# Attention of a decoder trunk on one Trainium2 core: score and value products of 256 columns as three passes over high and low parts, instead of plain fp32

## The chip, the core and the metric

The kernel runs on one core of a Trainium2 chip, as one launch. The metric is the device time of the whole launch in microseconds (us). Before the change it is 2285.92 us, the median of 3 runs from 2285.37 to 2287.04. A view of the profile names the engines so: PE is TensorE's matmuls and PEld its weight loads, DVE is VectorE, ACT is ScalarE, POOL is GpSimd, SP the queue that issues most DMAs.

## What is computed

256 tokens of width 2048 go through an attention mixer, an MLP, a state-space mixer and a second MLP, each with an RMS norm before it and a residual sum behind it. The change is in the attention mixer alone. What matters of its reference:

```python
q = (rms_norm(c_q, q_norm_g) @ w_uq).reshape(B, S, MLA_HEADS, QK_HEAD_DIM)      # 16 heads of 192
kv = (rms_norm(c_kv, kv_norm_g) @ w_ukv).reshape(B, S, MLA_HEADS, QK_NOPE_DIM + V_HEAD_DIM)
...
q = rms_norm(q, qn_g); k = rms_norm(k, kn_g)      # then rope on 64 of the 192 columns
s = jnp.einsum('bqhd,bkhd->bhqk', q_blk, k) * scale
mask = k_pos[None, :] <= q_pos[:, None]
p = jax.nn.softmax(jnp.where(mask, s, -jnp.inf), axis=-1)
return jnp.einsum('bhqk,bkhd->bqhd', p, v)
```

There are two blocks of 128 queries. The first sees 128 keys, the second 256, so that a head has score products of 128 and of 256 columns.

## The kernel before, in words

**Weights in two parts.** Nearly all matmul work of the kernel multiplies activations with weights, and both are held as two fp32r numbers, a high part (the value cut to fp32r) and a low part (the rest). A product is three passes: high by high, low by high, high by low (L339, L340, L343 in `block`; L616 to L618 in the MLPs). The parts of every weight chunk are made on the chip while the kernel runs: `halves` has ACT copy the chunk to fp32r (L102, tile `wh`) and DVE subtract that copy from the chunk (L103, `wl`). `Flow.convert` keeps this three chunks ahead of PE. So ACT and DVE have a steady load from the weights, beside what a mixer asks of them.

**The attention stage.** The 16 heads go in 8 units of two heads. The loop over the units in `mla_body` (L1018 and on) writes the work of several units into one another. Round u issues, in this order on PE: the query projection of unit u+1 (`s0q`, a block of 384 columns), the transposes of unit u-1's keys (`s1(u-1, "k")`), the key/value projection of unit u (`s0kv`, 512 columns) with the transposes of unit u-2's softmax in its middle (`s3`), the scores of unit u-1 (`s2`), the value products of unit u-2 (`s4`) and the transposes of unit u's queries (`s1(u, "q")`). Round 7 has a block of the output projection in place of `s0q`. PE keeps exactly the written order. A scheduler sets the order on ACT, DVE and POOL.

Between the stages a unit's data walks through the other engines:

- `q_stats`, `q_norm`: ACT squares and sums the projection (L296), POOL adds and takes the power -1/2 (L289, L290; called the root below), DVE scales it to `qn` (L887). `q_rope` on POOL turns 64 columns (L798 to L801) and copies `qn` by a DMA to fp32r words `qw`.
- `s0kv`, `k_norm`: the same for the keys: L296, the root on POOL, then DVE scales to `kn` (L916) and ACT adds the scaled rope part (L918). The values `v` are copied by ACT (L907).
- `s1`: PE transposes into PSUM banks, and DVE or ACT copies them out (L944, L946, L948) to plain fp32 tiles `qT` and `kT`. POOL clears the unused halves of the query tile (L927, L928).
- `s2`: per head, two products of 128 columns and two of 256 (L961, L962), plain fp32. DVE adds the mask and takes the maximum (L965), scales it (L967), ACT takes the exponential (L971), DVE the reciprocal (L972) and the product with it (L975).
- `s3`: three transposes per head, copied out by DVE (L987) for one head and ACT (L989) for the other.
- `s4`: per head one product of 256 columns (L997) and one of 128 (L998), plain fp32. `split_out` then makes the high part (ACT, L299) and the low part (DVE, L300) of the result for the output projection.

**Banks.** Transposes, scores and value products take their PSUM banks by turns from two pools, `yp` and `sm`, of two banks each, so that every fourth request gets the same bank again. The second bank of the key transposes is the one that `s4` of the round before wrote, and it is free once L300 has read it. Tiles of `xtp` (8) are shared by queries, keys, softmax and its transpose, four per unit.

Of the kernel before, what the change touches and what calls it, by code (L numbers as in the profile page):

```python
# [28 lines left out]
P = 128  # L29
# [185 lines left out]
class Trunk:  # L215
# [610 lines left out]
    def mla_body(self, mp, gain):  # L826
        nc, d = self.nc, self.d
        cq = [mp.tile([P, 4, 256], F32R, name=f"cq{i}") for i in range(2)]
        ckv = [mp.tile([P, 4, 256], F32R, name=f"ckv{i}") for i in range(2)]
        mk = mp.tile([P, 256], F32, name="mk")  # L830

        def setup():
            nc.gpsimd.memset(mk[:, 0:P], 0.0)
            nc.gpsimd.tensor_copy(mk[:, P:256], self.cst[:, C_MQ:C_MQ + P])
            self.rope_tables(mp)

# [2 lines left out]
        accs = self.block([("ain", "q", q) for q in range(4)], xT)  # L839
# [58 lines left out]

        def s0kv(u, mid=None):
            accs = self.block([("ukv", u)], ckvT, mid=mid)  # L900
            v = mp.tile([P, 2, 2, P], F32, tag="v", name=f"v{u}", bufs=3)
            ssq = self.stat(4)
            for t in range(2):
                for h in range(2):
                    self.square_sum(accs[t][:, h * P:(h + 1) * P], ssq[:, 2 * t + h:2 * t + h + 1], HD ** -0.5)
            for t in range(2):
                nc.scalar.activation(v[:, t].rearrange("p h f -> p (h f)"), accs[t][:, 256:512], AF.Copy)  # L907
            U[u]["kv"], U[u]["kr"], U[u]["v"] = accs, self.root(ssq, krss, 4), v

        def k_norm(u):  # L910
            accs, r = U[u]["kv"], U[u]["kr"]
# [9 lines left out]
        def s1(u, name):  # L921


            src, words = U[u][name + "n"], U[u].get(name + "w")
            dst = self.ktile(self.xtp, F32)
            if name == "q":
                nc.gpsimd.memset(dst[64:128, 2], 0.0)  # L927
                nc.gpsimd.memset(dst[0:64, 3], 0.0)  # L928
            for i in range(2):
                b = self.bank()  # L930
                parts = 2 - i
                for j in range(parts):
                    for t in range(2):
                        o = j * 256 + t * P
                        k = (2 * i + j) * P
                        if words is not None and (i, t) != (1, 1):
                            nc.tensor.transpose(b.bitcast(F32R)[:, o:o + P], words[:, t, k:k + P], self.ident_r)
                        else:
                            nc.tensor.transpose(b[:, o:o + P], src[:, t, k:k + P], self.ident)
                v = b[:, :parts * 256].rearrange("p (k n) -> p k n", k=parts)  # L940
                if i and name == "q":
                    for h in range(2):
                        r = slice(64 * h, 64 * h + 64)
                        nc.scalar.activation(dst[r, 2 + h], b[r, 0:256], AF.Copy)  # L944
                elif (i == 0) == (name == "q"):
                    nc.vector.tensor_copy(dst[:, 2 * i:2 * i + parts], v)  # L946
                else:
                    nc.scalar.activation(dst[:, 2 * i:2 * i + parts], v, AF.Copy)  # L948
            U[u][name + "T"] = dst

        def s2(u):
            qT, kT = U[u]["qT"], U[u]["kT"]
            p = self.ktile(self.xtp, F32).rearrange("p a b -> p (a b)")
            mx, nm, sm, rc = self.stat(4), self.stat(4), self.stat(4), self.stat(4)
            spans = ((0, P), (P, 384))
            for h in range(2):
                b = self.bank()
                q0, q1 = qT[:, h], qT[:, 2 + h]
                k0, k1 = kT[:, h], kT[:, 2]
                for o, n in ((0, P), (P, 256)):  # L960
                    nc.tensor.matmul(b[:, o:o + n], q0[:, o:o + P], k0[:, :n], start=True, stop=False)  # L961
                    nc.tensor.matmul(b[:, o:o + n], q1[:, o:o + P], k1[:, :n], start=False, stop=True)  # L962
                for i, (a, z) in enumerate(spans):
                    j = 2 * h + i
                    nc.vector.tensor_tensor_reduce(p[:, h * 384 + a:h * 384 + z], b[:, a:z], mk[:, 256 - (z - a):], 1.0, -3.0e38,  # L965
                                                   ALU.add, ALU.max, mx[:, j:j + 1])
                nc.vector.tensor_scalar(nm[:, 2 * h:2 * h + 2], mx[:, 2 * h:2 * h + 2], -SCALE, None, ALU.mult)  # L967
                for i, (a, z) in enumerate(spans):
                    j = 2 * h + i
                    v = p[:, h * 384 + a:h * 384 + z]  # L970
                    nc.scalar.activation(v, v, AF.Exp, bias=nm[:, j:j + 1], scale=SCALE, accum_out=sm[:, j:j + 1])  # L971
                nc.vector.reciprocal(rc[:, 2 * h:2 * h + 2], sm[:, 2 * h:2 * h + 2])  # L972
                for i, (a, z) in enumerate(spans):
                    j = 2 * h + i
                    nc.vector.tensor_scalar(p[:, h * 384 + a:h * 384 + z], p[:, h * 384 + a:h * 384 + z], rc[:, j:j + 1],  # L975
                                            None, ALU.mult)
            U[u]["p"] = p

        def s3(u):
            p = U[u]["p"]  # L980
            pT = self.ktile(self.xtp, F32).rearrange("p a b -> p (a b)")
            for h in range(2):
                b = self.bank()
                for i in range(3):
                    nc.tensor.transpose(b[:, i * P:(i + 1) * P], p[:, h * 384 + i * P:h * 384 + (i + 1) * P], self.ident)
                if h == 0:
                    nc.vector.tensor_copy(pT[:, 0:384], b[:, 0:384])  # L987
                else:
                    nc.scalar.activation(pT[:, 384:768], b[:, 0:384], AF.Copy)  # L989
            U[u]["pT"] = pT  # L990

        def s4(u):
            pT, v = U[u]["pT"], U[u]["v"]
            b = self.bank()
            for h in range(2):
                o = h * 256
                nc.tensor.matmul(b[:, o:o + 256], v[:, 0, h], pT[:, h * 384:h * 384 + 256], start=True, stop=False)  # L997
                nc.tensor.matmul(b[:, o + P:o + 256], v[:, 1, h], pT[:, h * 384 + 256:h * 384 + 384], start=False, stop=True)  # L998
# [609 lines left out]
```

## Time and profile before

| | |
|---|---|
| time of the runs | 2285.92 us median, 2285.37 to 2287.04 |
| the profiled execution, its own time | 2286.35 us |
| its span in the profile | 2284.5 us |
| granted TensorE clock | 1.0 of full speed |
| busy share of the span | PE 100%, PEld 83%, DVE 84%, ACT 61%, POOL 12% |
| the attention units, from the first scores to the last value products | about 83 to 210 us of the span |

A row of the timeline gives the start in us, the length in us, the engine, the source line, the operation, the tiles it writes and reads, the shape, and in brackets how long the engine stood idle before and what ended that. Instructions on one engine overlap a little in such rows (a matmul's or a copy's end lies behind the next one's start). What an instruction costs its engine in a full queue is therefore the distance from its start to the next start, which is called its step below. `x2` behind a row says that two instructions were merged into it. A plain fp32 matmul stands as two instructions in the trace.

### The profile page before, as it was taken

What the parts mean: (1) busy time and instruction counts of PE and PEld (TensorE: products, weight loads), DVE (VectorE), ACT (ScalarE), POOL (GpSimd) and SP (SyncE); (2) the same over time, 40 slices, a digit from 0 to 9 for tenths busy, and PEclk for the clock granted to TensorE, in tenths of its full rate; (3) what the DMA queues carried; (4) which work ended last, traced back from release to release, by engine and by line L of the source; (5) the groups of instructions that cost most, each with busy time, mean ns of one, the idle gap of its engine ahead of it and who ended that gap; (6) DMA issues with size and microseconds to landing.
All of it is one profiled execution on the core that took longest, in us unless ns stands there. A gap on an engine that the chain in (4) does not pass through costs nothing.

```text
span 2284.5 us, 30768 instructions
## 1 busy us (share of the span) xinstructions
PE 2278.1 (100%) x10929; PEld 1889.6 (83%) x10929; DVE 1915.9 (84%) x2318; ACT 1390.1 (61%) x1947; POOL 275.5 (12%) x315
## 2 busy tenths in 40 slices
PE   9999999999999999999999999999999999999999
PEld 7898888888888888888888888888888888888887
DVE  7786698999898897687899688676989889989985
ACT  7775576566666666564666555545666666666663
POOL 1440000000000000100133213121000000000000
PEclk9999999999999999999999999999999999999999
DMA  8545678888888878667888787767688888888874
GB/s 315 173 153 159 211 230 267 259 255 270 264 255 259 267 232 271 227 208 241 277 280 278 245 275 264 229 222 229 204 265 248 259 270 253 260 275 247 267 232 160
DMA packets 167706, 557.16 MB, mean 244 GB/s; under 512 B 19040, under 2 KB 28192, under 8 KB 166528
## 3 DMA queue, kind: packets, MB, share of 16 engines
q1 hardware_dynamic: 151264, 502.44, 66.2%
q0 software_dynamic: 13888, 48.49, 10.0%
q10 hardware_dynamic: 2400, 4.27, 0.5%
q8 instruction: 86, 1.41, 0.3%
q14 instruction: 68, 0.56, 0.1%
HBM read 529.65 MB, written 6.41 MB: 235 GB/s over the span
## 4 chain that ended last, share of the span: by engine, by line
PE 96%; DVE 1%; DMA 1%; ACT 1%; issue 1%; POOL 0%; SPq 0%; ACTq 0%; DVEq 0%
PE acc L339 13%; PE acc L340 13%; PE acc L343 13%; PE yp L618 9%; PE yp L617 9%; PE yp L616 9%; PE st L617 7%; PE st L618 7%; PE st L616 7%; DMA wraw<-mi 1%; PE sm L324 1%; DVE wl L103 1%; PE y L1309 1%; PE sm L322 1%; PE acc L616 1%; PE acc L618 1%
## 5 line engine op out<-in xcount | busy, mean ns | idle before, releaser
L102 ACT ACTIVATE wh<-wraw 128x1024 fp32r<-128x1024 f32 (+1 forms) x818 | 856.2, 1053 | 570.4 <-PE acc L340 268.9
L103 DVE TENSOR_TENSOR wl<-wraw,wh 128x1024 fp32r<-128x1024 f32 (+1 forms) x818 | 985.5, 1221 | 240.6 <-ACT wh L102 216.6
L616 PE MATMUL yp<-wh,k 128*128 128x512 f32 x896 | 349.2, 390 | 0.0
L618 PE MATMUL yp<-wh,k 128*128 128x512 f32 x896 | 348.8, 389 | 0.0
L617 PE MATMUL yp<-wl,k 128*128 128x512 f32 x896 | 348.6, 389 | 0.0
L339 PE MATMUL acc<-wh,xt 128*128 128x512 f32 x704 | 279.7, 397 | 0.4 <-ACT wh L102 0.4
L340 PE MATMUL acc<-wh,xt 128*128 128x512 f32 x704 | 274.9, 390 | 0.1
L102 ACT ACTIVATE wh<-wrx 128x1024 fp32r<-128x1024 f32 x168 | 177.8, 1058 | 153.4 <-PE yp L618 101.7
L103 DVE TENSOR_TENSOR wl<-wrx,wh 128x1024 fp32r<-128x1024 f32 x168 | 204.3, 1221 | 36.6 <-ACT wh L102 35.6
L618 PEld LDWEIGHTS yp<-wh,k 128*128 128x128 f32 x896 | 168.2, 188 | 35.1
L617 PEld LDWEIGHTS yp<-wl,k 128*128 128x128 f32 x896 | 168.2, 188 | 34.9
L616 PEld LDWEIGHTS yp<-wh,k 128*128 128x128 f32 x896 | 168.2, 188 | 34.8
L339 PE MATMUL acc<-wh,k 128*128 128x512 f32 x496 | 196.5, 396 | 0.0
L340 PE MATMUL acc<-wh,k 128*128 128x512 f32 x496 | 193.3, 390 | 0.0
L343 PE MATMUL acc<-wl,xt 128*128 128x512 f32 x704 | 188.3, 389 | 0.0
L616 PE MATMUL st<-wh,xt 128*128 128x512 f32 x448 | 177.7, 397 | 0.0
L618 PE MATMUL st<-wh,xt 128*128 128x512 f32 x448 | 174.9, 390 | 0.0
L617 PE MATMUL st<-wl,xt 128*128 128x512 f32 x448 | 174.7, 390 | 0.0
L339 PEld LDWEIGHTS acc<-wh,xt 128*128 128x128 f32 x704 | 132.7, 188 | 29.4 <-ACT wh L102 1.6
L340 PEld LDWEIGHTS acc<-wh,xt 128*128 128x128 f32 x704 | 132.5, 188 | 28.5 <-issue 1.2
L343 PEld LDWEIGHTS acc<-wl,xt 128*128 128x128 f32 x704 | 132.1, 188 | 27.7
L199 POOL DMA_DIRECT2D wrx<-mi x56 | 49.2, 878 | 720.6 <-DVE wl L103 524.5
(318 smaller groups left out, 3527.0 us busy)
## 6 DMA issues: line engine op xcount, KB each, us to landing
wraw<-mi SPq DMA_DIRECT2D x256, 512.0 KB, 5.5
wraw<-mo SPq DMA_DIRECT2D x256, 512.0 KB, 5.6
wraw<-si SPq DMA_DIRECT2D x160, 512.0 KB, 5.2
wraw<-so SPq DMA_DIRECT2D x64, 512.0 KB, 5.2
wrx<-mi SPq DMA_DIRECT2D x56, 512.0 KB, 5.4
wrx<-mi POOLq DMA_DIRECT2D x56, 512.0 KB, 7.8
wraw<-wo SPq DMA_DIRECT2D x32, 512.0 KB, 4.0
taps<-xD SPq DMA_DIRECT2D x16, 768.0 KB, 8.4
```

Source lines behind the costliest of these rows:

```text
L102: self.last = nc.scalar.activation(h[:, v], raw[:, v], AF.Copy)
L103: self.last_lo = nc.vector.tensor_tensor(lo[:, v], raw[:, v], h[:, v].bitcast(F32), ALU.subtract)
L199: nc.gpsimd.dma_start(st["b11"].tile, quarter(d, 1, 0), accum_op=ALU.add)
L322: self.nc.tensor.transpose(b.bitcast(F32R)[:, v], words[:, v], self.ident_r)
L324: self.nc.tensor.transpose(b[:, v], src[:, v], self.ident)
L339: nc.tensor.matmul(accs[t][:, :n], ah, wh[:, q, :], start=first and kt + q == 0, stop=False)
L340: nc.tensor.matmul(accs[t][:, :n], al, wh[:, q, :], start=False, stop=False)
L343: nc.tensor.matmul(accs[t][:, :n], lhs(kt + q, t)[0], wl[:, q, :], start=False, stop=en and q == nk - 1)
L616: nc.tensor.matmul(b, ah, wh, start=first and q == 0, stop=False)
L617: nc.tensor.matmul(b, ah, wl, start=False, stop=False)
L618: nc.tensor.matmul(b, al, wh, start=False, stop=last and q == 1)
L1309: nc.tensor.matmul(y[t][c, o], part(t)[:, c], xg[g][t][:, o], start=True, stop=True)
```

## The change

Every product of 256 columns in `s2` and `s4` becomes three fp32r passes over high and low parts. The products of 128 columns stay plain fp32. To feed both, the transposed queries, keys and softmax and the values are written out twice: the part that a plain product reads stays as an fp32 tile (`qraw`, `kraw`, `pT`, `v`), and what a 256-column product reads is written as a pair (`qhl`, `khl`, `phl`, `vhl`) by the new helper `parts`, an ACT copy to fp32r and a DVE subtraction. The two query tiles are allocated once for all units, with their unused halves cleared once, in place of two POOL memsets per unit.

```diff
+        qhl = mp.tile([P, 2, 4, P], F32R, name="qhl")
+        qraw = mp.tile([P, 4, P], F32, name="qraw")
         def setup():
             nc.gpsimd.memset(mk[:, 0:P], 0.0)
+            for q in (qhl[:, 0].bitcast(F32), qhl[:, 1].bitcast(F32), qraw):
+                nc.gpsimd.memset(q[64:128, 2], 0.0)
+                nc.gpsimd.memset(q[0:64, 3], 0.0)
...
+        def parts(h, lo, src):
+            nc.scalar.activation(h, src, AF.Copy)
+            nc.vector.tensor_tensor(lo, src, h.bitcast(F32), ALU.subtract)
...
         def s0kv(u, mid=None):
-            v = mp.tile([P, 2, 2, P], F32, tag="v", name=f"v{u}", bufs=3)
+            v = mp.tile([P, 2, P], F32, tag="v", name=f"v{u}", bufs=3)
+            vhl = mp.tile([P, 2, 2, P], F32R, tag="vhl", name=f"vhl{u}", bufs=3)
...
-            for t in range(2):
-                nc.scalar.activation(v[:, t].rearrange("p h f -> p (h f)"), accs[t][:, 256:512], AF.Copy)
+            parts(both(vhl[:, 0]), both(vhl[:, 1]), accs[0][:, 256:512])
+            nc.scalar.activation(both(v), accs[1][:, 256:512], AF.Copy)
...
         def s1(u, name):
-            dst = self.ktile(self.xtp, F32)
             if name == "q":
-                nc.gpsimd.memset(dst[64:128, 2], 0.0)
-                nc.gpsimd.memset(dst[0:64, 3], 0.0)
+                dst = qraw
+            else:
+                dst = mp.tile([P, 3, P], F32, tag="kraw", name=f"kraw{u}", bufs=1)
+                khl = [self.ktile(self.xtp) for _ in range(2)]
...
-                        nc.scalar.activation(dst[r, 2 + h], b[r, 0:256], AF.Copy)
-                elif (i == 0) == (name == "q"):
-                    nc.vector.tensor_copy(dst[:, 2 * i:2 * i + parts], v)
+                        nc.scalar.activation(dst[r, 2 + h], b[r, 0:P], AF.Copy)
+                        parts(qhl[r, 0, 2 + h], qhl[r, 1, 2 + h], b[r, P:256])
+                elif name == "q":
+                    nc.vector.tensor_copy(dst[:, 0:2], v[:, :, 0:P])
+                    parts(qhl[:, 0, 0:2], qhl[:, 1, 0:2], v[:, :, P:256])
                 else:
-                    nc.scalar.activation(dst[:, 2 * i:2 * i + parts], v, AF.Copy)
+                    nc.scalar.activation(dst[:, 2 * i:2 * i + parts_n], v[:, :, 0:P], AF.Copy)
+                    parts(khl[0][:, 2 * i:2 * i + parts_n], khl[1][:, 2 * i:2 * i + parts_n], v)
...
         def s2(u):
-                for o, n in ((0, P), (P, 256)):
-                    nc.tensor.matmul(b[:, o:o + n], q0[:, o:o + P], k0[:, :n], start=True, stop=False)
-                    nc.tensor.matmul(b[:, o:o + n], q1[:, o:o + P], k1[:, :n], start=False, stop=True)
+                nc.tensor.matmul(b[:, 0:P], q0[:, 0:P], k0[:, 0:P], start=True, stop=False)
+                nc.tensor.matmul(b[:, 0:P], q1[:, 0:P], k1[:, 0:P], start=False, stop=True)
+                for e, (i, k) in enumerate(((h, h), (2 + h, 2))):
+                    for f, (x, y) in enumerate(((0, 0), (0, 1), (1, 0))):
+                        nc.tensor.matmul(b[:, P:384], qhl[:, x, i], khl[y][:, k], start=e + f == 0, stop=e + f == 3)
...
         def s3(u):
-                if h == 0:
-                    nc.vector.tensor_copy(pT[:, 0:384], b[:, 0:384])
-                else:
-                    nc.scalar.activation(pT[:, 384:768], b[:, 0:384], AF.Copy)
+                parts(phl[:, 0, h], phl[:, 1, h], b[:, 0:256])
+                nc.scalar.activation(pT[:, h], b[:, 256:384], AF.Copy)
...
         def s4(u):
-                nc.tensor.matmul(b[:, o:o + 256], v[:, 0, h], pT[:, h * 384:h * 384 + 256], start=True, stop=False)
-                nc.tensor.matmul(b[:, o + P:o + 256], v[:, 1, h], pT[:, h * 384 + 256:h * 384 + 384], start=False, stop=True)
+                for f, (x, y) in enumerate(((0, 0), (0, 1), (1, 0))):
+                    nc.tensor.matmul(b[:, o:o + 256], vhl[:, x, h], phl[:, y, h], start=f == 0, stop=False)
+                nc.tensor.matmul(b[:, o + P:o + 256], v[:, h], pT[:, h], start=False, stop=True)
```

Lines behind 830 move down by 9 to 19 in the changed kernel: `parts` is L875 (ACT) and L876 (DVE), the key scaling L927 and L929, the mask L983, the scaled maximum L985, the exponential L989, the reciprocal L990, the product with it L993, the query scaling L896, the copy of the 64-row query parts L957, of the keys L963, of the softmax L1007.

**What the scheduler made of it on ACT**, from the exponentials of unit 2 to the statistics of unit 5's queries, a stretch that recurs with small shifts in rounds 3 to 6. Before:

```order
L971 ACTIVATE xt_1485,st_1488<-xt_1485,st_1487 128x256
L299 ACTIVATE k_61_716<-sm_1516 128x512
L944 ACTIVATE xt_1523<-sm_1532 64x256 x2
L102 ACTIVATE wh_1568<-wraw_1414 128x768
L102 ACTIVATE wh_1621<-wraw_1443 128x768
L296 ACTIVATE s_215_1585,st_1584<-acc_1546 128x192
```

and now:

```order
L989 ACTIVATE xt_1558,st_1561<-xt_1558,st_1560 128x256
L299 ACTIVATE k_61_724<-sm_1597 128x512
L875 ACTIVATE qhl<-yp_1608 128x256
L957 ACTIVATE qraw<-sm_1616 64x128
L875 ACTIVATE qhl<-sm_1616 64x128
L102 ACTIVATE wh_1656<-wraw_1480 128x768
L957 ACTIVATE qraw<-sm_1616 64x128
L875 ACTIVATE qhl<-sm_1616 64x128
L102 ACTIVATE wh_1715<-wraw_1514 128x768
L296 ACTIVATE s_214_1673,st_1672<-acc_1634 128x192
```

Two copies of 64 rows by 256 have become one of 128 by 256 and four of 64 by 128, spread around the weight chunks.

**On DVE**, from the scaling of unit 5's queries in round 4 to the masks behind it. Here `xt` is the low part of the keys (`_1687`) and of the softmax (`_1732`). Before:

```order
L103 TENSOR_TENSOR wl_1622<-wraw_1443,wh_1621 128x768
L946 COPY xt_1597<-sm_1604 128x256
L887 SCALAR_TENSOR_TENSOR qn_1608<-acc_1546,st_1594,cst 128x128
...
L887 SCALAR_TENSOR_TENSOR qn_1608<-acc_1547,st_1594,cst 128x64
L987 COPY xt_1637<-yp_1638 128x384
L103 TENSOR_TENSOR wl_1651<-wraw_1548,wh_1650 128x1024
L103 TENSOR_TENSOR wl_1756<-wraw_1566,wh_1755 128x1024
L965 ISA xt_1690,st_1691<-yp_1695,mk 128x128
```

and now:

```order
L103 TENSOR_TENSOR wl_1716<-wraw_1514,wh_1715 128x768
L896 SCALAR_TENSOR_TENSOR qn_1702<-acc_1634,st_1682,cst 128x128
L896 SCALAR_TENSOR_TENSOR qn_1702<-acc_1634,st_1682,cst 128x64
L876 TENSOR_TENSOR xt_1687<-yp_1688,xt_1686 128x512
L876 TENSOR_TENSOR xt_1687<-sm_1696,xt_1686 128x256
L896 SCALAR_TENSOR_TENSOR qn_1702<-acc_1634,st_1682,cst 128x128
...
L876 TENSOR_TENSOR xt_1732<-yp_1733,xt_1732 128x256
L876 TENSOR_TENSOR xt_1732<-sm_1740,xt_1732 128x256
L103 TENSOR_TENSOR wl_1750<-wraw_1636,wh_1749 128x1024
L103 TENSOR_TENSOR wl_1872<-wraw_1654,wh_1871 128x1024
L983 ISA xt_1791,st_1792<-yp_1796,mk 128x128
L983 ISA st_1792 128x1
L876 TENSOR_TENSOR vhl_1766<-acc_1711,vhl_1766 128x256
```

The copy of the second key bank, which stood ahead of the query scaling, is gone, and two subtractions for the keys stand between the first and the later query scalings. The one softmax copy of 384 columns has become two subtractions of 256, and the subtraction for the values follows the weight chunks.

More of the change, by code (lines that the diff above doesn't have):

```diff
@@ L905, in s0kv @@
                     self.square_sum(accs[t][:, h * P:(h + 1) * P], ssq[:, 2 * t + h:2 * t + h + 1], HD ** -0.5)
[L906 to L908 removed]
+            both = lambda w: w.rearrange("p h f -> p (h f)")
+            parts(both(vhl[:, 0]), both(vhl[:, 1]), accs[0][:, 256:512])
+            nc.scalar.activation(both(v), accs[1][:, 256:512], AF.Copy)
+            U[u]["kv"], U[u]["kr"], U[u]["v"] = accs, self.root(ssq, krss, 4), (v, vhl)
         def k_norm(u):
```

17 lines of the change are left out of this document (10 added, 7 removed).

## The prediction

> **What bounds the kernel now.** I read the page's busy times and its chain first, then the busy times by round in the attention stage, then single rows there.
>
> ```profile
> PE 2278.1 (100%) x10929; PEld 1889.6 (83%) x10929; DVE 1915.9 (84%) x2318; ACT 1390.1 (61%) x1947; POOL 275.5 (12%) x315
> PE 96%; DVE 1%; DMA 1%; ACT 1%; issue 1%; POOL 0%; SPq 0%; ACTq 0%; DVEq 0%
> ```
>
> PE is busy throughout, and the chain that ends last is PE for 96%. So a shorter PE stream shortens the kernel, if the other engines keep up. Whether they do must be read in the stage that changes. There the columns are the stretch, its length, then busy time and instructions of each engine:
>
> ```profile
> 113.50:128.94 15.44, 15.44 (x91) 14.04 (x90) 12.56 (x37) 11.47 (x40) 6.85 (x11) 1.00 0.44 148
> ```
>
> That is one round of the unit loop, from one `s2` to the next: PE never pauses in 15.44 us, while DVE and ACT seem to have 3 and 4 us to spare. They don't, as the next rows show: the first four are PE's second key transposes in rounds 2 to 5, the others DVE's subtraction (L300) that frees the bank for them.
>
> ```profile
> 107.08 0.44 PE L939 MATMUL yp<-ident,kn 128*128 128x128 f32 x2 [0.55 <-ACT xt L944]
> 122.55 0.38 PE L939 MATMUL sm<-ident,kn 128*128 128x128 f32 x2
> 137.99 0.38 PE L939 MATMUL yp<-ident,kn 128*128 128x128 f32 x2
> 153.43 0.38 PE L939 MATMUL sm<-ident,kn 128*128 128x128 f32 x2
> 106.40 0.69 DVE L300 TENSOR_TENSOR k<-yp,k 128x512 fp32r<-128x512 f32 x1 [0.32 <-ACT k L299]
> 121.75 0.69 DVE L300 TENSOR_TENSOR k<-sm,k 128x512 fp32r<-128x512 f32 x1 [0.32 <-ACT k L299]
> ```
>
> In round 2 PE stands 0.55 us, and L300 ends at 107.09, where PE goes on. (The row names ACT's L944, which ends there too; the bank is the one that L300 reads.) In round 3 L300 ends at 122.44 and PE starts at 122.55. So PE passes this point 0.1 us behind DVE, and DVE's rounds are 15.35 us apart, PE's 15.44. **A second loop through ACT, POOL and DVE is as long as PE's own round.** One turn of it, in order of time:
>
> ```profile
> 117.24 1.07 ACT L918 ACTIVATE kn<-kro,st 128x64 f32<-128x64 f32 x4 [1.81 <-POOL st L290]
> 118.21 0.39 ACT L971 ACTIVATE xt<-xt,st 128x128 f32<-128x128 f32 x1
> 120.24 0.40 ACT L971 ACTIVATE xt<-xt,st 128x128 f32<-128x128 f32 x1 [1.06 <-DVE kn L916]
> 121.14 0.58 ACT L299 ACTIVATE k<-sm 128x512 fp32r<-128x512 f32 x1
> 121.62 0.76 ACT L944 ACTIVATE xt<-sm 64x256 f32<-64x256 f32 x2
> 122.40 1.58 ACT L102 ACTIVATE wh<-wraw 128x768 fp32r<-128x768 f32 x2
> 124.01 0.33 ACT L296 ACTIVATE s<-acc 128x192 f32<-128x192 f32 x1
> 125.24 0.61 ACT L948 ACTIVATE xt<-yp 128x512 f32<-128x512 f32 x1
> 126.79 1.89 DVE L887 SCALAR_TENSOR_TENSOR qn<-acc,st,cst 128x128 f32<-128x128 f32 x8 [1.35 <-POOL st L290]
> 128.60 0.55 DVE L987 COPY xt<-yp 128x384 f32<-128x384 f32 x1
> 129.06 2.35 DVE L103 TENSOR_TENSOR wl<-wraw,wh 128x1024 fp32r<-128x1024 f32 x2
> 130.39 1.08 POOL L289 TENSOR_TENSOR st<-st,krss 128x4 f32<-128x4 f32 x1 [3.63 <-ACT s L296]
> 131.33 0.28 DVE L965 CUSTOM_DVE_ANT_0 xt<-yp,mk 128x128 f32<-128x128 f32 x1
> 132.59 0.35 DVE L916 SCALAR_TENSOR_TENSOR kn<-acc,st,cst 128x128 f32<-128x128 f32 x1 [0.63 <-POOL st L290]
> ```
>
> By distances of starts: key rope 0.97, first exponentials and the wait for the second maximum 2.03, second exponentials 0.90, `split_out` 0.48, query copies 0.78, two weight chunks 1.61, query statistics 1.23, the root on POOL 1.55 (125.24 to 126.79), query scaling 1.81, softmax copy 0.46, two weight chunks on DVE 2.27, and from their end to the key scaling 1.26. The sum is 15.35, the whole turn. The last step is there because POOL's small addition (L289) does not get through while DVE's two subtractions run:
>
> ```profile
> 98.37 2.35 DVE L103 TENSOR_TENSOR wl<-wraw,wh 128x1024 fp32r<-128x1024 f32 x2
> 98.77 2.01 POOL L289 TENSOR_TENSOR st<-st,krss 128x4 f32<-128x4 f32 x1 [2.71 <-ACT s L296]
> ```
>
> It starts 0.4 us into the pair and takes 2.01 us, to the pair's end; 0.19 us is its time elsewhere. The Trainium skill, "SBUF — State Buffer", section "SBUF: two separate sides", says that VectorE and GpSimd take one port pair as an exclusive lock for a whole instruction. By that rule alone POOL would get in between the two subtractions, the root would come up to 1.14 us earlier and the loop would fall under PE's round (the second rival's time); the row shows that it waited through both.
>
> **The change, part by part.** PE first: plain products of 256 columns, and the fp32r passes of the same size in the narrow projection.
>
> ```profile
> 97.76 0.60 PE L961 MATMUL yp<-xt,xt 128*128 128x256 f32 x2
> 98.63 0.38 PE L961 MATMUL sm<-xt,xt 128*128 128x128 f32 x2
> 99.94 0.59 PE L997 MATMUL yp<-xt,v 128*128 128x256 f32 x2
> 100.37 0.38 PE L998 MATMUL yp<-xt,v 128*128 128x128 f32 x2
> 31.05 2.08 PE L358 MATMUL sm<-xt,wl 128*128 128x256 f32 x16
> 32.97 0.40 PE L339 MATMUL acc<-wh,xt 128*128 128x512 f32 x1
> ```
>
> Two plain score products take 0.87 us, one value product 0.43. Sixteen passes of 256 columns take 1.92 us, 0.12 each, every one with its own weight load. There are 8 units x 2 heads x (2 + 1) = 48 such products: 48 x 0.435 = 20.9 us become 144 x 0.12 = 17.3. **PE saves 3.6 us**, 0.45 a unit, and its round becomes 14.99. The Trainium skill, "FP8 and Floating Point Precision", section "TensorE Precision Notes", counts a true fp32 product as four passes; by that rule three passes would save a quarter, 5.2 us. The measured pass (0.12) is dearer than a quarter of 0.435, so the sum goes by the row.
>
> Now the loop. Its new instructions have no exact row. The nearest ones are these, with L918, L944 and L887 above:
>
> ```profile
> 114.76 0.67 ACT L907 ACTIVATE v<-acc 128x256 f32<-128x256 f32 x2
> 120.60 0.68 DVE L946 COPY xt<-yp 128x512 f32<-128x512 f32 x1
> 125.02 0.42 DVE L946 COPY xt<-sm 128x256 f32<-128x256 f32 x1
> ```
>
> An ACT copy of 256 columns has a step of 0.29 (the pair's 0.67 less the last one's 0.38). For a 64x128 copy the rows bound 0.24 (the 64 columns of L918) and 0.39 (64x256, L944); I take 0.25, being nearer in size to the first. A DVE subtraction that reads 512 columns of PSUM takes 0.60 (a step of L300, like L946's 0.68 less 0.08 overlap); for 256 the bounds are 0.26 (a 128-column scaling) and 0.60, and I take 0.34, by L946's 0.42 less the overlap. What the loop now holds:
>
> - The query copies on ACT: 0.78 becomes 0.29 + 4 x 0.25 = 1.29, so +0.51.
> - The key subtractions, between the query scalings: +0.60 + 0.34. The L946 of 256 columns that they replace ran in DVE's wait for the root, so nothing comes off.
> - The softmax: 2 x 0.34 in place of 0.46, +0.22.
> - The wait inside the exponentials, 1.13 (2.03 less the 0.90 that the second pair takes), goes: the second head's maximum now stands ahead of the key scaling on DVE, and the POOL memset beside which L967 was held is gone. -1.13; the other end is that it stays, 0.
> - The value subtraction and the remaining ACT copies run where DVE or ACT waited for the root: 0. Their cover is 0.63 us on DVE and 1.81 on ACT; without it they cost 0.34 and about 0.3.
>
> The sum is 15.35 + 0.54 = **15.89 us**, against PE's 14.99. So PE does not keep its gain inside the loop; it waits about 0.9 us a round. What counts is how late the loop gets, and that starts before it is steady. The key roots now:
>
> ```profile
> 75.04 1.02 POOL L290 TENSOR_TENSOR st<-st,mhalf 128x4 f32<-128x4 f32 x1
> 85.73 1.01 POOL L290 TENSOR_TENSOR st<-st,mhalf 128x4 f32<-128x4 f32 x1
> 100.86 1.01 POOL L290 TENSOR_TENSOR st<-st,mhalf 128x4 f32<-128x4 f32 x1
> 162.42 1.01 POOL L290 TENSOR_TENSOR st<-st,mhalf 128x4 f32<-128x4 f32 x1
> 170.18 0.38 PE L939 MATMUL yp<-ident,kn 128*128 128x128 f32 x2
> ```
>
> Those are rounds 0, 1, 2 and 6, then PE's second key transposes of round 7. Round 0 to 1 gets the key subtractions (0.94) and two of the four short copies (0.50): +1.44. Round 1 to 2 has no wait to lose, so it gets 0.94 + 0.22 + 0.51 = +1.67. Rounds 2 to 6 are four turns of +0.54. The root of round 6 is 5.3 us late, at 167.7. Behind it in DVE's new order the last scaling of unit 6's keys comes only after L300 and the first two query subtractions: 1.04 to the end of the root, 0.97 + 1.80 + 0.48 on ACT, then 0.15 + 0.60 + 0.34 + 0.21 + 0.36 on DVE, and 0.44 for the first transposes. PE's second ones start at 167.7 + 6.4 = 174.1, 3.9 us later than at 170.18. From there on round 7 and the tail have blocks of the output projection where ACT and DVE have time, so PE saves in full: two scores at 0.30 and three value products at 0.15, 1.05 us. **Net +2.9 us**: 2286.35 + 2.9 = 2289.2 for the profiled execution. That one lies 0.43 above the median of the runs, so the time I forecast is 2288.8. Behind the attention PE bounds as before, and the MLPs and the state-space part have the same instructions.
>
> **Rivals.**
>
> 1. *The wait inside the exponentials stays* (slower). L967 is a tiny DVE instruction that the rows of POOL's rope hold up, and the rope still runs there, 2.3 us behind each root. For it: the wait is in every round of before, and now two DVE scalings of maxima fall into the rope. Against it: the memset at its end is gone. Each 0.1 us of wait costs 0.4 us over four turns; from 0.45 us on the kernel is slower by over 0.2%. At the full 1.13 it is 2.9 + 4.5 = +7.4 us, 2293.3. Short copies at 0.39 instead of 0.25 lead to the same place (4 x 0.56 + 0.28 = +2.5 more).
> 2. *The loop keeps pace.* If POOL gets in between two DVE subtractions, or ACT and DVE fill their waits better, the turn stays under 14.99, and PE keeps 3.6 us: 2282.3. Even then it is not faster by over 0.2% (4.6 us), unless the 0.55 us of round 2 and the waits of rounds 0 and 1 go as well. Against it: the 2.01 us row, and a turn that already fills 15.35 of 15.44.
> 3. *The passes don't cost 0.12*: with high and low parts changing at every pass, PE could be held by the weight loads, 0.19 us each as a row of its own. 144 x 0.19 = 27.4, 6.5 more than now: 2292.4 if all else is hidden. Against it: L358 loads at every pass too.
>
> **How the numbers follow.** I give the forecast, a loop that costs 0 to 4.6 us in all, 0.50; the first rival 0.36; the second 0.12; the third 0.02. What a measurement of this kernel can tell from no change is about 0.2%, 4.6 us. Slower by more: 0.36 + 0.02 = 0.38. Faster by more: 0.02, a part of the second rival. Within: 0.60. The range takes in most of the second rival below and the first one with part of the dear copies above: 2283.5 to 2295; the likeliest case alone is 2286 to 2290.5.
>
> **What would show it right or wrong.** Right: in rows of the profile after, 144 passes of 256 columns 0.12 apart; PE standing 0.5 to 1.5 us ahead of the key transposes in rounds 2 to 7, released by DVE; roots of rounds 2 to 5 some 15.9 us apart; ACT and DVE nearly without a pause between roots but for the root itself. Wrong: roots less than 15.3 apart or PE without a pause (second rival), a bracket of over 0.5 us ahead of the second exponentials (first), or a difference that lies behind 215 us, where nothing changed.

## The result and the profile after

| | before | after |
|---|---|---|
| time of the runs, median | 2285.92 us (2284.44 to 2288.32, 9 runs) | 2292.24 us (2290.87 to 2293.82, 9 runs) |
| ratio, 95% interval | | 1.0026 (1.0016 to 1.0036) |
| the profiled execution, its own time | 2286.35 us | 2291.24 us |
| its span | 2284.5 us | 2289.4 us |
| key roots of rounds 0 and 6 | 75.04, 162.42 | 74.78, 168.53 |

The changed kernel is slower by 6.3 us (3.7 to 8.2 by the interval). The forecast was 2288.8, so the time is 3.4 us above it. It lies in the range of 2283.5 to 2295, but past the likeliest case's own range (2286 to 2290.5). By the median it is also past the 0.2%, to which 0.38 had been given; the interval reaches below that.

First the page's busy times and the shares of the chain that ended last:

```profile
PE 2275.2 (99%) x10977; PEld 1888.6 (82%) x10977; DVE 1921.8 (84%) x2366; ACT 1403.0 (61%) x2019; POOL 269.6 (12%) x305
...
PE 95%; DVE 2%; ACT 1%; DMA 1%; issue 1%; POOL 0%; SPq 0%; ACTq 0%; DVEq 0%; POOLq 0%
```

PE is busy 2.9 us less than before (2278.1), and the span is 4.9 us longer: PE now stands still for some 14 us in place of 6. Where it stands in the attention tells the list of PE's waits from 60 to 215 us (line, what released it, total us, times, longest):

```profile
PE yp L950 <- DVE st L983: 2.9, 3, 1.5
PE sm L950 <- DVE st L983: 1.5, 2, 1.1
PE sm L952 <- DVE kn L927: 1.3, 1, 1.3
PE yp L952 <- DVE kn L927: 0.9, 1, 0.9
PE yp L1016 <- ACT pT L1007: 0.6, 1, 0.6
PE yp L952 <- DVE qn L896: 0.4, 1, 0.4
PE sm L1005 <- DVE qhl L876: 0.4, 1, 0.4
```

Together 8.0 us; before, the same stage had 0.41 and 0.55. Most of it, 4.4 us, stands at the query transposes (L950), in rows like these of rounds 5 and 6:

```profile
152.90 0.28 PE L950 MATMUL sm<-ident,qw 128*128 128x128 f32 x1 [1.09 <-DVE st L983]
169.30 0.28 PE L950 MATMUL yp<-ident,qw 128*128 128x128 f32 x1 [1.11 <-DVE st L983]
```

Their second bank is the one that held the first head's scores four requests before, and it comes free when DVE's masks (L983) have read it. The prediction had looked at the key transposes' bank alone.

The products themselves cost what was forecast. Six score passes, three value passes, and the first passes of the second head:

```profile
117.62 0.96 PE L980 MATMUL sm<-xt,qhl 128*128 128x256 f32 x6
118.78 0.96 PE L980 MATMUL yp<-xt,qhl 128*128 128x256 f32 x6
...
119.58 0.52 PE L1016 MATMUL sm<-xt,vhl 128*128 128x256 f32 x3
```

From one head to the next it is 1.16 us, of which the two plain products of 128 columns take 0.44, so 0.12 a pass.

The second loop is read off POOL's key roots, one a round (before they were 10.69, 15.13, 15.34, 15.35, 15.34 and 15.53 apart):

```profile
74.78 1.02 POOL L290 TENSOR_TENSOR st<-st,mhalf 128x4 f32<-128x4 f32 x1
...
87.00 1.01 POOL L290 TENSOR_TENSOR st<-st,mhalf 128x4 f32<-128x4 f32 x1
...
103.61 1.01 POOL L290 TENSOR_TENSOR st<-st,mhalf 128x4 f32<-128x4 f32 x1
...
119.54 1.01 POOL L290 TENSOR_TENSOR st<-st,mhalf 128x4 f32<-128x4 f32 x1
...
135.70 1.01 POOL L290 TENSOR_TENSOR st<-st,mhalf 128x4 f32<-128x4 f32 x1
...
152.10 1.01 POOL L290 TENSOR_TENSOR st<-st,mhalf 128x4 f32<-128x4 f32 x1
...
168.53 1.01 POOL L290 TENSOR_TENSOR st<-st,mhalf 128x4 f32<-128x4 f32 x1
```

They are now 12.22, 16.61, 15.93, 16.16, 16.40 and 16.43 apart. One turn, from the key scaling at 120.58 to the next at 136.75, in rows of ACT, then of DVE and POOL:

```profile
120.58 1.07 ACT L929 ACTIVATE kn<-kro,st 128x64 f32<-128x64 f32 x4 [0.85 <-POOL st L290]
121.56 0.39 ACT L989 ACTIVATE xt<-xt,st 128x128 f32<-128x128 f32 x1
...
122.43 0.39 ACT L989 ACTIVATE xt<-xt,st 128x128 f32<-128x128 f32 x1
...
123.31 0.57 ACT L299 ACTIVATE k<-sm 128x512 fp32r<-128x512 f32 x1
123.79 0.36 ACT L875 ACTIVATE qhl<-yp 128x256 fp32r<-128x256 f32 x1
124.05 0.26 ACT L957 ACTIVATE qraw<-sm 64x128 f32<-64x128 f32 x1
124.21 0.26 ACT L875 ACTIVATE qhl<-sm 64x128 fp32r<-64x128 f32 x1
...
125.46 0.27 ACT L957 ACTIVATE qraw<-sm 64x128 f32<-64x128 f32 x1 [0.25 <-DVE qhl L876]
...
132.75 0.28 ACT L1007 ACTIVATE pT<-yp 128x128 f32<-128x128 f32 x1 [1.91 <-DVE xt L876]
...
133.26 1.05 ACT L102 ACTIVATE wh<-wraw 128x1024 fp32r<-128x1024 f32 x1
134.21 0.27 ACT L296 ACTIVATE s<-acc 128x128 f32<-128x128 f32 x1
...
136.75 1.07 ACT L929 ACTIVATE kn<-kro,st 128x64 f32<-128x64 f32 x4 [0.86 <-POOL st L290]
```

```profile
129.56 0.54 DVE L896 SCALAR_TENSOR_TENSOR qn<-acc,st,cst 128x128 f32<-128x128 f32 x2 [1.70 <-POOL st L290]
130.02 0.68 DVE L876 TENSOR_TENSOR xt<-yp,xt 128x512 fp32r<-128x512 f32 x1
130.62 0.41 DVE L876 TENSOR_TENSOR xt<-sm,xt 128x256 fp32r<-128x256 f32 x1
130.95 1.44 DVE L896 SCALAR_TENSOR_TENSOR qn<-acc,st,cst 128x128 f32<-128x128 f32 x6
132.31 0.41 DVE L876 TENSOR_TENSOR xt<-yp,xt 128x256 fp32r<-128x256 f32 x1
132.63 0.41 DVE L876 TENSOR_TENSOR xt<-sm,xt 128x256 fp32r<-128x256 f32 x1
132.97 1.21 DVE L103 TENSOR_TENSOR wl<-wraw,wh 128x1024 fp32r<-128x1024 f32 x1
...
135.42 0.21 POOL L289 TENSOR_TENSOR st<-st,krss 128x4 f32<-128x4 f32 x1 [5.89 <-ACT s L296]
```

The second exponentials follow the first without a bracket: the wait there has gone. New are two brackets on ACT. The copies L957 and L1007 read a bank that DVE's subtraction reads too, and each goes on when that subtraction is done (L1007 at 132.75, the subtraction's end at 132.72), though both only read. Behind L1007 on ACT stand a weight chunk (L102) and the key statistics (L296), on which the next key root depends. POOL's addition for that root is no longer held up: it takes 0.21 us here, 1.08 in the turn before the change.

### The profile page after: what moved, and what is told of

It is laid out like the page before. It is cut to its first block, busy times and chain, and to the rows that moved or that the text cites. A ratio compares the mean times of both kernels' runs of the same rounds, so it can differ in the third digit from the quotient of the medians.

```text
span 2289.4 us, 30983 instructions
## 1 busy us (share of the span) xinstructions
PE 2275.2 (99%) x10977; PEld 1888.6 (82%) x10977; DVE 1921.8 (84%) x2366; ACT 1403.0 (61%) x2019; POOL 269.6 (12%) x305
## 4 chain that ended last, share of the span: by engine, by line
PE 95%; DVE 2%; ACT 1%; DMA 1%; issue 1%; POOL 0%; SPq 0%; ACTq 0%; DVEq 0%; POOLq 0%
PE acc L339 13%; PE acc L340 13%; PE acc L343 13%; PE yp L617 9%; PE yp L618 9%; PE yp L616 9%; PE st L617 7%; PE st L618 7%; PE st L616 7%; DVE wl L103 1%; PE sm L324 1%; PE y L1328 1%; PE sm L322 1%; PE acc L616 1%; PE acc L618 1%; PE acc L617 1%
## 5 line engine op out<-in xcount | busy, mean ns | idle before, releaser
L102 ACT ACTIVATE wh<-wraw 128x1024 fp32r<-128x1024 f32 (+1 forms) x818 | 857.1, 1053 | 563.1 <-PE acc L340 260.8
L102 ACT ACTIVATE wh<-wrx 128x1024 fp32r<-128x1024 f32 x168 | 177.8, 1058 | 153.7 <-PE yp L618 102.0
```

The lines of the kernel that those rows point to most:

```text
L102: self.last = nc.scalar.activation(h[:, v], raw[:, v], AF.Copy)
```

## The experiments

Each time is a median of the runs, with the ratio to the kernel before on the same chip, which took 2286.07 to 2286.24 beside the experiments. "Root 0 to 6" is the distance from the first to the seventh key root in the trace, six turns of the loop.

| run | us | ratio, 95% interval | root 0 to 6, us |
|---|---|---|---|
| before | 2285.92 | | 87.38 |
| after | 2292.24 | 1.0026 (1.0016 to 1.0036) | 93.75 |
| plain_pe | 2292.01 | 1.0026 (1.0016 to 1.0036) | 93.74 |
| no_low | 2285.80 | 0.9999 (0.9990 to 1.0008) | 84.38 |
| act_first | 2288.86 | 1.0013 (1.0004 to 1.0022) | 90.63 |
| after_recip | 2282.51 | 0.9987 (0.9978 to 0.9995) | - |
| scores_only | 2289.25 | 1.0015 (1.0006 to 1.0023) | 91.38 |
| values_only | 2288.41 | 1.0008 (0.9999 to 1.0017) | 88.85 |
| before_recip | 2284.25 | 0.9993 (0.9984 to 1.0001) | - |
| twice_sub | 2292.24 | 1.0026 (1.0016 to 1.0036) | 93.20 |
| before_step | 2288.63 | 1.0011 (1.0003 to 1.0020) | 89.83 |
| root_step | 2294.57 | 1.0037 (1.0024 to 1.0049) | 95.74 |
| values_act_first | 2285.52 | 0.9997 (0.9988 to 1.0006) | 85.91 |
| values_cleared | 2285.26 | 0.9997 (0.9988 to 1.0006) | 85.85 |

Where the six turns are longer than before's 87.38, the time follows them roughly one to one: +2.45 and +2.5 us (before_step), +3.25 and +2.8 (act_first), +4.0 and +3.2 (scores_only), +5.8 and +6.2 (twice_sub), +6.36 and +5.9 (plain_pe), +6.37 and +6.3 (after), +8.36 and +8.4 (root_step), each against the kernel before beside it. values_only fits worst, with +1.5 and +2.3. Where the turns are shorter, PE leads and little comes of it.

The scheduler answers most edits with another order, so that few of these runs change one thing alone. Counted are the instructions that stand outside the longest order which two traces share. Against before, before_step has none on ACT and DVE. Against the changed kernel, root_step has 3 on ACT and 13 on DVE, plain_pe 11 and 26, act_first 32 and 34. On ACT, 16 of act_first's are the softmax copies that it turns round. Against values_only, values_act_first has just those 16 on ACT and 10 on DVE. Where many have moved, the time is that of the edit and of the new order together.

**plain_pe: the loop as in the change, PE's work as before.** The high parts alone are multiplied, as plain fp32; all copies and subtractions stay.

```diff
-                    for f, (x, y) in enumerate(((0, 0), (0, 1), (1, 0))):
-                        nc.tensor.matmul(b[:, P:384], qhl[:, x, i], khl[y][:, k], start=e + f == 0, stop=e + f == 3)
+                    nc.tensor.matmul(b[:, P:384], qhl[:, 0, i].bitcast(F32), khl[0][:, k].bitcast(F32), start=e == 0, stop=e == 1)
...
-                for f, (x, y) in enumerate(((0, 0), (0, 1), (1, 0))):
-                    nc.tensor.matmul(b[:, o:o + 256], vhl[:, x, h], phl[:, y, h], start=f == 0, stop=False)
+                nc.tensor.matmul(b[:, o:o + 256], vhl[:, 0, h].bitcast(F32), phl[:, 0, h].bitcast(F32), start=True, stop=False)
```

> The changed kernel with its 256-column products plain fp32 on the high parts, all copies and subtractions kept (the low parts are computed and left out of the products). Theory, the loop through ACT, DVE and POOL sets the pace: PE gets 3.6 us more work, but has waited 6.9 us for masks and keys in rounds 1 to 7 and takes most of it from there, so 2292 to 2294 us. Rival, the time is lost on PE or its passes: all 3.6 us show, 2296 us, or with dear passes it gets faster than 2292.

Measured 2292.01, the same as the changed kernel within 0.3 us. Its page shows PE with the work of before:

```profile
PE 2278.4 (100%) x10929; PEld 1889.2 (83%) x10929; DVE 1925.9 (84%) x2366; ACT 1403.0 (61%) x2019; POOL 271.5 (12%) x305
```

PE has as many instructions as before (10929) and is busy 3.2 us longer than in the changed kernel (2275.2), and the roots are as far apart as there. So in the changed kernel no gain of PE's that can be told reaches the end.

**no_low: the subtractions left out.** The three passes read the high parts each time; what the low parts add is missing from the result. (The cut shows the helper alone; the products' operands change with it.)

```diff
         def parts(h, lo, src):
             nc.scalar.activation(h, src, AF.Copy)
-            nc.vector.tensor_tensor(lo, src, h.bitcast(F32), ALU.subtract)
```

> The changed kernel without the subtractions on DVE (the low parts are left out, each of the three passes reads the high parts). Theory: the loop loses the key subtractions 0.93, the softmax subtractions 0.66 and the ACT waits for them, about 0.4 us a turn, 16.17 becomes about 14.2, under PE's 14.99, so PE keeps its 3.6 us and loses its old waits: 2281.5 to 2283.5 us. Rival, the added ACT copies alone hold PE: 2288 us or more.

Measured 2285.80, 6.4 us less than the changed kernel, but 2.3 us over what was expected. In the attention it did as the theory says: the last value product starts at 206.53, against 210.11 before and 214.70 in the changed kernel, and PE keeps its full 3.6 us. Of these, 3.1 are lost behind the attention (the span is 2284.0 us, 2284.5 before); 2.15 of them stand in the second MLP, at three places where PE waits for the low part of a weight chunk:

```profile
1818.82 0.50 PE L617 MATMUL st<-wl,sN 128*128 128x512 f32 x1 [0.76 <-DVE wl L103]
1903.10 0.50 PE L617 MATMUL st<-wl,sN 128*128 128x512 f32 x1 [0.62 <-DVE wl L103]
2070.75 0.50 PE L617 MATMUL st<-wl,sN 128*128 128x512 f32 x1 [0.77 <-DVE wl L103]
```

DVE's waits there say what was late (no_low first, then before, from 1540 to 2260 us):

```profile
DVE wraw L183 <- DMA wraw<-mi: 14.6, 12, 2.3
```

```profile
DVE wraw L183 <- DMA wraw<-mi: 8.1, 14, 1.6
```

The transfers of the weights came later against the rest of the work than before, while the instructions behind the attention stand in the same order. Why they do so in this kernel and hardly in after_recip, which is earlier still (0.26 us of such waits), stays open. Being early is not the cause by itself: such waits stand at a like place in kernels that run later (0.77 us at 2076.30 in twice_sub, 0.63 at 2073.38 in values_only), and each trace is one execution.

**act_first: ACT's plain copies ahead of DVE's subtraction.**

```diff
                         nc.scalar.activation(dst[r, 2 + h], b[r, 0:P], AF.Copy)
-                        parts(qhl[r, 0, 2 + h], qhl[r, 1, 2 + h], b[r, P:256])
+                        nc.scalar.activation(qhl[r, 0, 2 + h], b[r, P:256], AF.Copy)
+                    for h in range(2):
+                        r = slice(64 * h, 64 * h + 64)
+                        nc.vector.tensor_tensor(qhl[r, 1, 2 + h], b[r, P:256], qhl[r, 0, 2 + h].bitcast(F32), ALU.subtract)
...
-                parts(phl[:, 0, h], phl[:, 1, h], b[:, 0:256])
                 nc.scalar.activation(pT[:, h], b[:, 256:384], AF.Copy)
+                parts(phl[:, 0, h], phl[:, 1, h], b[:, 0:256])
```

> The changed kernel with the ACT copies out of a bank issued ahead of the DVE subtraction from it (softmax and 64-row query parts); nothing is left out. Theory, part of the turn is ACT waiting for DVE's read of the same bank (0.25 and 0.16 us of 16.17, and the softmax copy that holds a weight chunk back): 0.3 to 0.5 us a turn go, 2289.5 to 2291 us. Rival, those waits lie beside the root on POOL and DVE's queue: no change, 2292 us.

Measured 2288.86, 3.4 us less than the changed kernel and a little better than expected. ACT's waits in the changed kernel, of which both are gone here:

```profile
ACT pT L1007 <- DVE xt L876: 10.6, 8, 1.9
...
ACT qraw L957 <- DVE qhl L876: 1.0, 3, 0.5
```

So more than half of the change's cost goes with this edit. How much of the 3.4 us the two waits are by themselves isn't shown, since the scheduler also moved other instructions, and one turn got a new wait: 1.82 us for DVE's scaled maximum at 120.59, ahead of the exponentials. values_act_first against values_only, below, is the cleaner test.

**after_recip and before_recip: a short root.** The addition and a reciprocal on DVE take the place of POOL's addition and power; the square root is left out.

```diff
-        self.nc.gpsimd.tensor_tensor(v, mean, more, ALU.add)
-        self.pow = self.nc.gpsimd.tensor_tensor(r, v, self.mhalf[:, :n], ALU.pow)
+        self.nc.vector.tensor_tensor(v, mean, more, ALU.add)
+        self.pow = self.nc.vector.reciprocal(r, v)
```

> The changed kernel with the root of the query and key statistics as an addition and a reciprocal on DVE in place of POOL's addition and power (the square root is left out). Theory: a turn holds two of these roots, 1.54 and 1.27 us; at 0.4 each it falls by about 2 us to 14.2, under PE's round of 14.99, so 2281.5 to 2284 us. Rival, another wait takes its place (masks behind the weight chunks in DVE's queue): 2289 us or more.

> The kernel before with the root as an addition and a reciprocal on DVE (the square root is left out, as in the changed kernel's run of the same kind, 2282.5). Theory: before, PE bounds its rounds and the loop is just as long, so a shorter loop brings only PE's waits in the attention, 0.4 and 0.55 us, and little more: 2284.7 to 2285.5. The two runs with the shorter root are then 2.2 to 3 us apart, PE's 3.6 less what is left of waits. Rival (the root's own work, not the loop's length, made the changed kernel faster by 9.7): also near 2276 to 2282.

With the change 2282.51, 9.7 us less; without it 2284.25, only 1.8 less, which its interval doesn't tell from the kernel before. The first is as the theory has it, the second a little under its range, and they are 1.7 us apart where 2.2 to 3 were expected. By the spans (2280.0 and 2282.4) it is 2.4 us, near the 2.8 of PE's saving less two waits of 0.35 and 0.46 us that the first still has in the attention. The traces show the saving itself: between 111 and 157 us of the span PE's rounds, from one `s2` to the next, are 15.00 to 15.01 us with the change and 15.44 without, against 14.99 and 15.44 in the prediction. So with the loop out of the way PE leads in both kernels, and the change makes its rounds shorter.

**scores_only and values_only: one half each.** In the first, values and softmax are as before; in the second, queries, keys and scores are.

```diff
-                parts(phl[:, 0, h], phl[:, 1, h], b[:, 0:256])
-                nc.scalar.activation(pT[:, h], b[:, 256:384], AF.Copy)
-            U[u]["pT"] = pT, phl
+                if h == 0:
+                    nc.vector.tensor_copy(pT[:, 0:384], b[:, 0:384])
+                else:
+                    nc.scalar.activation(pT[:, 384:768], b[:, 0:384], AF.Copy)
+            U[u]["pT"] = pT
```

(That is the softmax in scores_only; values and `s4` go back in the same way, and values_only puts `s1` and `s2` back.)

> Only the score products are three passes; values and softmax are copied and multiplied as before (plain fp32). Theory (the loop through ACT, POOL and DVE sets the pace): the query copies and the key subtractions stay in the loop, the second softmax subtraction (0.2 us a turn) and ACT's wait for DVE's read of the softmax bank (up to 0.4 us a turn by what it holds back) go. Over four steady turns and the two early ones that is 1 to 3 us less than the changed kernel: 2289 to 2291. Rival (the lateness is that of the softmax copies alone): about 2284, with PE's 2.4 us for the scores kept.

> Only the value products are three passes; queries, keys and scores are as before (plain fp32). Theory (loop): PE's round is 0.29 us shorter (15.15), the loop's turn 15.35 before gets 0.2 us for the second softmax subtraction and 0 to 0.4 us by ACT's wait at the softmax bank, so the loop leads and PE keeps nothing: 2286 to 2288.5. Rival (each product's saving counts by itself): 2284.7, 1.2 us less than before.

Measured 2289.25 and 2288.41, both within what the theory expected, the second at the upper end. The halves cost 3.2 and 2.3 us, together a little less than the whole (6.3).

**twice_sub: one subtraction on the loop done twice.**

```diff
                     parts(khl[0][:, 2 * i:2 * i + parts_n], khl[1][:, 2 * i:2 * i + parts_n], v)
+                    if i:
+                        nc.vector.tensor_tensor(khl[1][:, 2:3], v, khl[0][:, 2:3].bitcast(F32), ALU.subtract)
```

> The changed kernel with its second key subtraction (256 columns, 0.33 us on DVE) done twice in each unit, with the same result. Theory (loop): the extra one lies on the loop between the query scalings, so six or seven turns get 0.33 us each: 2.0 to 2.4 us more, 2294.2 to 2294.6. Rival (DVE has room in its waits, and the lateness comes from ACT alone): within 0.6 us of the changed kernel, 2291.7 to 2292.8.

Measured 2292.24, no more than without it: the theory missed. The trace shows the subtraction in its place between the query scalings (L966, a step of 0.34), but also another order on ACT, chosen by the scheduler: a weight chunk now stands ahead of the plain softmax copies (L1009 here).

```profile
131.92 1.06 ACT L102 ACTIVATE wh<-wraw 128x1024 fp32r<-128x1024 f32 x1 [1.47 <-PE acc L340]
132.88 0.26 ACT L1009 ACTIVATE pT<-yp 128x128 f32<-128x128 f32 x1
```

ACT's wait for DVE there is 4.1 us in place of 10.6, and the roots are as far apart as without the extra work. So this run adds a cost and takes one away, and says nothing of the first alone. The next two were meant to leave the order as it is.

**before_step and root_step: the root made longer.** A small copy on POOL between the addition and the power of every root, in the kernel before and in the changed one.

```diff
         self.nc.gpsimd.tensor_tensor(v, mean, more, ALU.add)
-        self.pow = self.nc.gpsimd.tensor_tensor(r, v, self.mhalf[:, :n], ALU.pow)
+        w = self.stat(n)
+        self.nc.gpsimd.tensor_copy(w, v)
+        self.pow = self.nc.gpsimd.tensor_tensor(r, w, self.mhalf[:, :n], ALU.pow)
```

> The kernel before with one more small copy on POOL (128x4) between the addition and the power of every root; the result and the order on the other engines are the same. POOL's addition has a step of 0.26 us, so each root should come 0.26 us later and the loop's turn, which holds two roots, should grow by 0.5 us, from 15.35 to 15.9. Theory (loop and PE were level before): the rounds follow the loop, 0.4 us late each over six or seven turns, 2.2 to 3.3 us more: 2288.2 to 2289.4. Rival (PE has cover for a later root): within 0.6 us of before, 2285.5 to 2286.7.

> The changed kernel with the same extra copy on POOL in every root. Theory (loop): all of the 0.5 us a turn shows, since the loop leads already; the key roots come 16.7 us apart instead of 16.2, and the time is 3 to 3.6 us more over six or seven turns: 2295.2 to 2295.9. Rival (the lateness comes from the order of ACT's and DVE's queues, which has room behind a later root, as the run with the subtraction done twice would have it): within 1 us, 2291.2 to 2293.2.

In the kernel before, where the orders of PE, ACT and DVE don't change at all, it costs 2.5 us (2288.63, against 2286.17 beside it): as expected. Two steps of 0.26 us in a turn show, on an engine that is busy 12% of the time. In the changed kernel, where 16 instructions on DVE and ACT change places, it costs 2.3 us (2294.57) where 3 to 3.6 were expected; the last three turns are 16.67 to 16.71, some 0.3 us longer than without it, not 0.5. The direction holds and the size doesn't; whether the changed order took the rest was not tried.

**values_act_first and values_cleared: the best of what was found.** Value products alone as passes, with ACT's plain copy first; then also one query tile, cleared once.

```diff
-                parts(phl[:, 0, h], phl[:, 1, h], b[:, 0:256])
                 nc.scalar.activation(pT[:, h], b[:, 256:384], AF.Copy)
+                parts(phl[:, 0, h], phl[:, 1, h], b[:, 0:256])
```

> Value products alone as three passes, with ACT's plain copy of a softmax bank ahead of the copy and subtraction for the pair, so that ACT doesn't wait there for DVE's read. Theory: of the 2.3 us that the value products cost when done alone (2288.4), the part by ACT's wait goes: 1 to 2 us, 2286.4 to 2287.4. Rival (the second softmax subtraction alone makes it): 2288.4 as without it.

> Value products alone as three passes, ACT's plain copy first, and in addition one query tile for all units whose unused halves are cleared once (as the change does), in place of two POOL memsets a unit; the result is the same. Theory: the loop's turn is under PE's round already, so what is left to gain is one wait of PE of 0.44 us and little stretches that the profile doesn't list: 2284.5 to 2285.5, at most 1 us less than without it (2285.5). Rival (the memsets still hold DVE's scaling of the maxima up and with it the loop): 2283 to 2284.3, at which point this version is faster than the kernel before.

Measured 2285.52, 2.9 us less than values_only and more than the 1 to 2 expected: ACT's wait at the softmax copies (13.4 us in all in values_only, none here) goes, and with it as much as the whole cost. ACT's order changes by the swapped copies alone, DVE's by 10 instructions, so this is the cleanest price on record of the order of the two reads. In the attention PE has no wait left behind 102 us of the span, and the turns from there on are 14.4 to 15.3. Clearing the query tile once brought nothing that can be told (2285.26). Neither is told apart from the kernel before by its interval. No version with a full root was found that is.

## Why the prediction was right, and where not

The mechanism was right: a second loop takes the lead and PE's gain is lost in it. The time was not near the forecast. It lies in the range because the range had room for the first rival and for dear copies, not because the sum led there.

- **PE's saving**: right. 0.12 a pass in the rows, and 0.44 us a round between the two kernels with the short root, where 0.45 was worked out. The 3.2 us between the busy times of plain_pe and the changed kernel say less, since the changed kernel's PE instructions have busy times from 2273.8 (after_recip) to 2276.7 us (act_first). The Trainium skill, "FP8 and Floating Point Precision", section "TensorE Precision Notes", counts four passes for a true fp32 product, which gave the estimate of 5.2; the rows decide against it here.
- **The second loop takes the lead and PE keeps nothing inside it**: right, by plain_pe, after_recip against before_recip, and the distances of the roots.
- **Loop and PE were level before**: right, by before_step.
- **The wait inside the exponentials goes**: right in the turn shown. The first rival came near in size (+6.3, it had +7.4) but not by its mechanism; two such waits, 0.24 and 1.51 us, stand at 186 and 202 us, behind the loop, and none inside it.
- **The query copies, +0.51**: too dear in themselves, since a copy of 64x128 has a step of 0.15 to 0.18, not 0.25. ACT's wait among them (L957, 0.25 us here and 0.48 in the next turn), which the prediction didn't have, makes up for it and more: with the two weight chunks it is 3.00 us to the query statistics (123.79 to 126.79), 3.24 in the next turn, where 2.90 were summed.
- **The key subtractions, 0.94, and the softmax's, 0.22**: as forecast, 0.93 and 0.20 in the turn.
- **"The value subtraction and the remaining ACT copies run where DVE or ACT waited for the root: 0"**: this is the step that failed. ACT's plain softmax copies don't wait for the root, they wait for DVE's subtraction from the same bank, up to 1.91 us, and hold back a weight chunk and the key statistics. The end of the turn, costed at 1.26 for POOL's blocked addition, is now ACT's: from the end of the softmax subtractions to the next key scaling it is 3.78 us (132.97 to 136.75), where the two chunks and POOL's wait were 3.53 before. In act_first, where ACT doesn't wait there, it is 3.53 again (131.79 to 135.32). So of a wait of 1.91 us the turn pays 0.25. With the wait among the query copies the later turns are 16.16 to 16.43 and not 15.89, and the seventh root is 6.1 us late, not 5.3. Without both waits the time is 3.4 us less (act_first), though with other instructions moved as well.
- **Where PE waits**: wrong place. The bank that the masks (L983) free holds up the query transposes, ahead of the keys' bank. That changes where PE stands and not what the loop's turn costs.
- **The tail, 1.05 us saved**: 0.69 from the second key transposes of round 7 (175.46) to the last value product (214.70), since PE waits 0.39 once more at L950 in between. Behind it 0.3 us are lost in the profiled execution, where PE waits 0.38 us at 2075.69 and 0.40 at 2162.10.

In the profiled execution the sum is then 5.3 us late at the key transposes (3.9 forecast), less 0.7, plus 0.3: 4.9 of span, where 2.9 were forecast. Of the 1.4 us too little at the key transposes, 0.8 had come by the root of round 6, and 0.5 lie between it and PE's second ones (6.93 us where 6.4 were summed; L300 stands there behind a product of the softmax on DVE). The medians lie 1.4 us further apart than the two profiled executions: the one before lies 0.43 us above its median, as the prediction had it, the one after 1.0 below.

## What to carry to other kernels

An engine that is 96% of the chain of waits need not be what a change must spare: if a loop through other engines has the same period, work that is moved off the first onto the second lengthens the kernel, and a small dose on the least busy engine (0.26 us on POOL) told it here in one run. When one bank is copied out by two engines, look which of them the program lets go first, also where both only read. And a dose, or a cure, has a price of its own only if the order of the other instructions stays.

## What the runs showed that had not been expected

- Two engines that only read one PSUM bank were put one behind the other by the program: ACT waited 10.6 us in all over 8 softmax copies. Turning the two round took 3.4 us off the changed kernel (act_first, with other instructions moved) and 2.9 off values_only (values_act_first, with few).
- A copy of 64x128 from PSUM on ACT has a step of 0.16 us (124.05 to 124.21), against 0.26 for 128x256 (123.79 to 124.05).
- POOL's small copy and addition each have a step of 0.26 us, its power 1.0; the addition and the reciprocal on DVE are 0.16 and 0.18 us long in a query root (after_recip).
- In no_low 3.1 of the 3.6 us gained in the attention were lost behind it, 2.15 of them at three weight chunks 1600 to 1900 us later; the cause stays open.
